# The taps of two channel tiles as four token phases on TensorE, and the second modulation columns on VectorE

## The chip, the cores and the metric

The kernel runs on one core of a Trainium2 chip. A core has TensorE (PE, the matrix multiplies), VectorE (DVE), ScalarE (ACT), GpSimd (POOL) and SyncE (SP), which mostly issues DMAs; POOL issues DMAs too. The metric is the device time of one execution in microseconds (us).

## The reference

Two residual layers on 1024 tokens of 1024 channels, then one RMSNorm. Layer 0 mixes tokens with a convolution module, layer 1 with sliding means; each is followed by a SwiGLU feed-forward part. The change lies in layer 0:

```python
def modulate(h, shift, scale):
    return h * (1.0 + scale[:, None, :]) + shift[:, None, :]

def conformer_conv(h, w1, b1, w_dw, b_dw, ln_g, ln_b, w2, b2):
    u = h @ w1 + b1
    a, g = jnp.split(u, 2, axis=-1)
    u = a * jax.nn.sigmoid(g)
    u = lax.conv_general_dilated(u, w_dw[:, None, :], window_strides=(1,),
        padding=[(CONV_WIDTH - 1, 0)], feature_group_count=D_MODEL) + b_dw
    u = jax.nn.silu(layer_norm(u, ln_g, ln_b))
    return u @ w2 + b2

    mod = c_act @ ada_w[i] + ada_b[i]          # c_act = silu(c), 6 x 1024 values
    sh_m, sc_m, g_m, sh_f, sc_f, g_f = jnp.split(mod, N_ADA, axis=-1)
    h = modulate(rms_norm(x, norm_mix_g[i]), sh_m, sc_m)
    ...
    x = x + (1.0 + g_m)[:, None, :] * y
    h = modulate(rms_norm(x, norm_ffn_g[i]), sh_f, sc_f)
    y = swiglu_ffn(h, ffn_w_gate[i], ffn_w_up[i], ffn_w_down[i])
    x = x + (1.0 + g_f)[:, None, :] * y
```

So each channel of the gated values `u` is convolved along the tokens with its own 31 taps (CONV_WIDTH). The layer norm over channels needs the taps of all channels of a token, and the feed-forward part's input `h` needs the scale `sc_f`.

## The kernel before

Channels lie on the 128 partitions, tokens along the free axis. There are two token chunks of 512, A and B, and eight channel tiles of 128, 0 to 7. A float32 product is made of three matmuls: each operand is split into a high and a low part, and `products` multiplies high by high, high by low and low by high. A weight is loaded by SP into a `raw` tile (3 buffers) and split into a `w` tile (5 buffers). ACT makes the high part (CAST w<-raw). For the low part a "summed" weight lets ACT write the negative copy (ACTIVATE w<-raw), to which a DMA of POOL's queue adds the weight again (w<-in_...); a "direct" one lets DVE subtract (TENSOR_TENSOR w<-raw,w).

Layer 0 in the order of PE's matmuls, by the names of their outputs: `a` and `g` are the two halves of `h @ w1` of one tile and chunk; first all of chunk A, and tiles 6 and 7 of B with those of A; then B's tiles 0 and 1; then `tap`, the taps that PE does; then B's tiles 2 to 5 with chunk A's layer norm between them (`mean`, `var`, `rstd`, one matmul or eight small ones each); `y`, the product with w2 for chunk A; B's last tile, and in it the norm of the feed-forward part for A (`var`, `rstd` again); then `p`, the first products of the feed-forward part, which read that norm's `h`.

The taps of a tile and chunk are 31 multiply-adds of shifted copies. VectorE does them into an accumulator `ca`; ACT and POOL share them (`pr` is a product by ACT, POOL sums into `pa`); a class `Taps` hands them out. Of chunk A PE does all 31 taps of tile 7 and 15 of tile 6: a tap there is a diagonal 128 x 128 weight (six weights `wdg` of up to eight diagonals), three matmuls of 482 to 512 columns, 138 in all. ACT reads tile 7's result from PSUM and adds the bias (u<-tap,vecs); tile 6's is added to VectorE's part. Chunk B's taps of both tiles are done by VectorE, ACT and POOL.

The modulation of layer 0 comes in columns, j = 0 to 5. For j = 2, 3 and for the second set, j = 4, 5 (the feed-forward scale and gate), PE multiplies `c` by the loaded columns (`ada`, `ada_columns`): of a column's eight row blocks, four matmuls each; two blocks are 16 records in the trace (each matmul counts twice), called a pair below; and at a column's end two transposing matmuls (`adac`). Other columns are done by VectorE in "dots" (`ada_task`): the loaded 128 x 1024 block times `cact`, summed along the free axis into one column of `mod`, eight dots a column. `adaw` tiles have 2 buffers (ADA_BUFS), so a load waits for the use of the one two before it. Behind column 4, POOL adds the bias and makes the scale (`mod`, `gains`); the first operation of the norm, t<-x,gains,rstd, reads it.

PE runs in the order in which the program is written; on the other engines a scheduler sets the order from the program, its priorities and manual dependencies. A planner keeps a clock for each engine; `pace` gives out steps of the waiting tasks to VectorE and POOL up to where PE's clock stands. `finish` and units such as `scale_done` force a task to its end. `mean_rsqrt` makes a norm's root (about eight small VectorE operations on `col` and `var`); operations in the list `recent`, the last 6 dots among them (RECENT), get a manual dependency that puts them behind the root.

Of the kernel before, what the change touches and what calls it, by code (L numbers as in the profile page):

```python
# [52 lines left out]
PE_TAPS = {6: 15, 7: CW}  # L53
# [46 lines left out]


def tap_groups(p):

    n = PE_TAPS[p]

    todo = list(range(CW - 1, -1, -1) if n == CW else range(CW - 3, CW - 3 - 2 * n, -2))
    return [todo[i : i + DIAGS] for i in range(0, len(todo), DIAGS)]
# [26 lines left out]
def trunk(ctx, tc, xT, c, vec, ada, adan, w1f, w1, wdg, w2, wgu, wdn, wds, wpl, out):  # L134
# [210 lines left out]
    kinds_d = [{q: [dram.tile([P, 2, 2, 512], F32, name=f"kinds_{l}_{q}_{b}") for b in range(3)] for q in BY_SEVEN[l]} for l in range(DEPTH)]  # L345
    KINDS = {"t1": (0, 0), "b22": (0, 1), "t3": (1, 0), "t2": (1, 1), "b11": (2, 0), "t4": (2, 1)}
# [55 lines left out]
    def ada_task(l, js, pause=None, first=None):  # L402

        def gen():
            todo = [(j, k) for j in js for k in range(KT)]
            ws = [ada_load(ada[(l * 6 + j) * KT + k], soft) for j, k in todo[:ADA_BUFS]]
            for i, (j, k) in enumerate(todo):
                yield first if first and i == 0 else pause or ("next" if "pooled" in st else "slow")
                ada_dot(ws.pop(0), l, j, k)
                if i + ADA_BUFS < len(todo):  # L410
                    j2, k2 = todo[i + ADA_BUFS]
                    ws.append(ada_load(ada[(l * 6 + j2) * KT + k2], soft))
                if k == KT - 1:
                    ada_post(l, j, 0, KT, G_)
                    ada_done.add((l, j))
# [324 lines left out]
    def conv_glu(ch, p, ba, bg, own=False):  # L740
        u = st["u", ch.i, p]
# [21 lines left out]
    def conv_in(*todo, fine=4):  # L763

        def emit(take):
            got = {}
            for each in todo:
# [4 lines left out]
                conv_u(ch, p)  # L772
# [10 lines left out]
                if ch.i == 0 and PE_TAPS.get(p, 0) < CW:  # L783
                    T["taps", 0, p] = Taps(A, p)
                if ch.i == 0 and p == KT - 1:
                    for q in PE_TAPS:
                        if PE_TAPS[q] < CW:
                            split_u(q)
# [3 lines left out]
    def split_u(p):  # L792

        u = st["u", 0, p][:, HALO - 2 : HALO - 2 + A.n]
        hi, lo = st["us", p] = pair("h0", "us")
        S_.copy(hi, u)
        either(A.n).tensor_tensor(lo, u, hi.bitcast(F32), op=SUB)

    def pe_taps(p):


        groups = tap_groups(p)
        us = []
        for i, js in enumerate(groups):
            def emit(take, i=i, js=js):
                if i == 0:
                    st["tap", p] = bank("tap")
                b, wt = st["tap", p], take()
                for q, j in enumerate(js):
                    full = PE_TAPS[p] == CW  # L810
                    o = (CW - 1 - j) // 2 * 2 if full else CW - 3 - j
                    c = j + o if full else 0
                    products(b[:, o:], wt, q, [v[:, c : c + A.n - o] for v in st["us", p]], j == groups[0][0], j == groups[-1][-1])
                    if q % 4 == 3:
                        pace()
                if i == len(groups) - 1:
                    if full:
                        S_.activation(st["u", 0, p][:, HALO:], b, AF.Identity, bias=V("conv_bdw", p))
                        st["taps", 0][p] = True
                    else:  # L820
                        T["taps", 0, p].other = b
            us.append((emit, wdg[sum(len(tap_groups(q)) for q in PE_TAPS if q < p) + i]))
        return us

    class Taps:
# [5 lines left out]
        def __init__(self, ch, p):  # L831
            self.ch, self.p, self.done, self.urgent = ch, p, False, False
            self.acc, self.part, self.other = None, None, None

            others = tap_groups(p) if ch.i == 0 and p in PE_TAPS else []
            self.todo, self.awaits = [j for j in range(CW - 1) if not any(j in js for js in others)], bool(others)
            tasks.append(self)

        def step(self, e):
# [43 lines left out]
            if e != "V" or self.awaits and self.other is None:  # L883
# [5 lines left out]
            if self.awaits:  # L889
                V_.tensor_tensor(d, d, self.other, op=ADD)  # L890
# [1136 lines left out]
    unit(lambda take: finish(*(T["taps", 0, p] for p in range(KT) if PE_TAPS.get(p, 0) < CW)))  # L2027
# [229 lines left out]
```

## Time and profile before

| | |
|---|---|
| time, median of 3 runs | 1676.87 us (1676.09 to 1678.81) |
| profiled execution, its own time | 1675.66 us |
| its span | 1673.9 us |
| PE busy | 1651.8 us (99%), 7550 matmul records |
| DVE, ACT, POOL busy | 1310.0 (78%), 804.1 (48%), 487.4 us (29%) |
| DMA | 378.60 MB, mean 226 GB/s |

A row of a timeline reads: start, duration, engine, line, operation, output<-inputs, the shape, the count, and in brackets the idle time ahead of it with what ended it. Rows of a kind that overlap or follow at once are joined into one with a count; its duration reaches from the first start to the last end, and a matmul's end is modelled, so the start of the next row says more than the sum of durations. L151 and L128 are helpers that record every operation, so groups are told apart by the names of tiles. The table by stages gives for each engine the busy time and the count. A row on a DMA issue gives the size and the median time from issue to landing.

### The profile page before, as it was taken

How to read it: one execution, taken by the hardware profiler on the slowest of the kernel's cores; microseconds unless marked ns; L12 is line 12 of the kernel's file. 1: busy time of each engine (PE TensorE's matmuls, PEld its weight loads, DVE VectorE, ACT ScalarE, POOL GpSimd, SP SyncE). 2: the span in 40 equal slices, each digit the busy share in tenths (PEclk: the TensorE clock that was granted, in tenths of full speed). 3: DMA queues.
4: the chain of work that ended last, by engine and by line, in shares of the span. 5: the costliest groups of instructions: out<-in, count | busy, mean ns of one | idle time of the engine just before them, and what ended most of it. 6: DMA issues, size and time to landing. Idle time of an engine off the chain costs nothing.

```text
span 1673.9 us, 21194 instructions
## 1 busy us (share of the span) xinstructions
PE 1651.8 (99%) x7550; PEld 1351.2 (81%) x7550; DVE 1310.0 (78%) x1867; ACT 804.1 (48%) x1090; POOL 487.4 (29%) x567
## 2 busy tenths in 40 slices
PE   7999999999999999999999999999999999999997
PEld 5777878787888888888888888888888888888887
DVE  8889899799759888888678957848777766658657
ACT  3669696867546332332234436637322222244354
POOL 3587777796002111221100502101111111000013
PEclk9999999999999999999999999999999999999999
DMA  8958997828776888886965959866777776686664
GB/s 301 295 176 228 225 236 205 226 78 241 229 234 168 278 264 287 282 272 206 400 231 164 285 155 283 247 211 199 189 225 222 220 227 183 207 273 207 192 170 126
DMA packets 117180, 378.60 MB, mean 226 GB/s; under 512 B 12369, under 2 KB 14545, under 8 KB 117074
## 3 DMA queue, kind: packets, MB, share of 16 engines
q1 hardware_dynamic: 79664, 245.63, 41.6%
q0 software_dynamic: 36832, 131.09, 32.5%
q8 instruction: 59, 0.97, 0.2%
q10 hardware_dynamic: 578, 0.53, 0.1%
q14 instruction: 47, 0.39, 0.1%
HBM read 310.61 MB, written 62.39 MB: 223 GB/s over the span
## 4 chain that ended last, share of the span: by engine, by line
PE 88%; POOL 3%; DVE 2%; DMA 2%; issue 2%; ACT 2%; DVEq 0%; SPq 0%; POOLq 0%; ACTq 0%
PE a L151 24%; PE dn L151 23%; PE e L151 14%; PE p L151 10%; PE y L151 6%; POOL pa L128 3%; PE first L151 3%; PE g L151 2%; PE tap L151 2%; DMA adaw<-in_adan_dram 1%; DMA s<-in_wds_dram 1%; PE ada L151 1%; ACT w L128 1%; DMA w<-in_wgu_dram 1%; PE var L151 1%
## 5 line engine op out<-in xcount | busy, mean ns | idle before, releaser
L128 ACT CAST w<-raw 128x1024 fp32r<-128x1024 f32 (+1 forms) x247 | 254.6, 1033 | 305.5 <-PE dn L151 56.9
L128 DVE TENSOR_TENSOR w<-raw,w 128x1024 fp32r<-128x1024 f32 (+1 forms) x173 | 209.3, 1214 | 62.2 <-ACT w L128 61.9
L151 PE MATMUL a<-n,w 128*128 128x512 f32 x1056 | 246.8, 389 | 0.2
L151 PE MATMUL p<-h,w 128*128 128x512 f32 x1056 | 243.7, 390 | 1.2 <-DMA w<-in_wgu_dram 1.0
L128 POOL TENSOR_TENSOR pa<-pa,pr 128x512 f32<-128x512 f32 x159 | 225.3, 1500 | 29.0 <-ACT pr L128 23.7
L151 PEld LDWEIGHTS p<-h,w 128*128 128x128 f32 x1056 | 197.3, 188 | 43.7 <-DMA w<-in_wgu_dram 1.4
L151 PEld LDWEIGHTS a<-n,w 128*128 128x128 f32 x1056 | 198.0, 188 | 42.2 <-DVE r L128 1.1
L151 PE MATMUL dn<-hi,w 128*128 128x512 f32 (+1 forms) x768 | 226.2, 377 | 0.4 <-DVE w L128 0.4
L151 PE MATMUL dn<-g,w 128*128 128x512 f32 x864 | 199.1, 390 | 0.2 <-DVE x L128 0.2
L151 PEld LDWEIGHTS dn<-g,w 128*128 128x128 f32 x864 | 161.7, 188 | 34.7 <-DVE x L128 0.6
L128 DVE SCALAR_TENSOR_TENSOR ca<-u,vecs,ca 128x512 f32<-128x512 f32 x246 | 170.6, 747 | 0.5
L151 PEld LDWEIGHTS dn<-hi,w 128*128 128x128 f32 x768 | 141.2, 188 | 27.0 <-DVE w L128 0.9
L151 PE MATMUL dn<-lo,w 128*128 128x512 f32 (+1 forms) x384 | 144.3, 376 | 0.0
L151 PE MATMUL a<-t,w 128*128 128x512 f32 x528 | 123.3, 389 | 0.0
L151 PE MATMUL e<-t,w 128*128 128x512 f32 x528 | 123.3, 389 | 0.0
L151 PE MATMUL e<-b,w 128*128 128x512 f32 x528 | 123.3, 389 | 0.0
L128 ACT ACTIVATE pr<-u,vecs 128x512 f32<-128x512 f32 x159 | 108.4, 717 | 25.0 <-POOL pa L128 19.7
L151 PEld LDWEIGHTS a<-t,w 128*128 128x128 f32 x528 | 99.1, 188 | 20.7
L151 PEld LDWEIGHTS e<-t,w 128*128 128x128 f32 x528 | 99.1, 188 | 20.6
L151 PEld LDWEIGHTS e<-b,w 128*128 128x128 f32 x528 | 99.1, 188 | 20.6
L1191 POOL DMA_DIRECT2D raw<-in_wgu_dram x41 | 36.5, 889 | 271.5 <-DVE r L128 104.2
L128 ACT CAST hi<-op 128x1024 fp32r<-128x1024 f32 (+1 forms) x52 | 48.5, 935 | 87.1 <-PE dn L151 77.2
(191 smaller groups left out, 2449.4 us busy)
## 6 DMA issues: line engine op xcount, KB each, us to landing
raw<-in_wgu_dram SPq DMA_DIRECT2D x132, 512.0 KB, 4.7
raw<-in_wds_dram SPq DMA_DIRECT2D x48, 512.0 KB, 6.0
adaw<-in_ada_dram POOLq DMA_DIRECT2D x48, 512.0 KB, 6.8
kinds<-k POOLq DMA_DIRECT2D x42, 512.0 KB, 7.7
raw<-in_wgu_dram POOLq DMA_DIRECT2D x41, 512.0 KB, 7.3
raw<-in_w_dram SPq DMA_DIRECT2D x36, 512.0 KB, 6.6
op<-kinds SPq DMA_DIRECT2D x36, 512.0 KB, 4.8
adaw<-in_adan_dram SPq DMA_DIRECT2D x32, 512.0 KB, 5.5
```

The lines of the kernel that those rows point to most:

```text
L128: self.last = self.order(getattr(self.eng, name)(out, *args, **kw))
L151: last_mm[0] = nc.tensor.matmul(out, lhsT, rhs, start=start, stop=stop, skip_group_check=more).ins.name
L1191: d = order(nc.gpsimd.dma_start(w[i], wgu[l, fp, src], accum_op=ADD))
```

## The change

**Taps.** PE now does all 31 taps of tiles 6 and 7, for both chunks. The tokens of a tile are dealt out in four phases (token modulo 4), and a matmul's 128 rows are 4 phases of 32 channels; so a tile gives four groups of 32 channels with 256 columns (1024 tokens / 4) each. A weight holds for each channel a 4 x 4 table of taps, from phase to phase, and nine shifts by a column (NM) cover the 31 taps: 2 tiles x 4 groups x 9 = 72 weight blocks, 9 `wdg` weights of eight, three matmuls of 256 columns for each block, 216 in all. Of the 9 weights those with even numbers are direct, the others summed.

The data changes its place through DRAM: the gated values go into a tile `ny` ordered by phase, by one DMA to `phased_d`; four or eight DMAs bring them into `us` with the phases on partitions; ACT makes the high part and DVE the low one. Results are copied by ACT into `acc`, stored to `tapped_d`, loaded by four DMAs for each tile and chunk into `ny`, and ACT's activation puts them back in order with the bias. All these DMAs are SP's. B's tile 0 now stands ahead of the taps on PE, tile 1 behind them; the return of B's tiles 6 and 7 is a unit behind tile 1. `Taps` no longer handles tiles 6 and 7.

**Modulation.** The second set, j = 4 and 5, is no longer PE's: `ada_task` makes 16 dots on VectorE of it, with loads on SP's queue.

```diff
-PE_TAPS = {6: 15, 7: CW}
+ON_PE = (6, 7)
+PHASES = 4
+GC = P // PHASES
+NM = (CW - 1 + 2 * (PHASES - 1)) // PHASES
+LEAD = NM - 1
+SEG = 2 * WSLOT // PHASES
 DIAGS = 8
...
-    def ada_task(l, js, pause=None, first=None):
+    def ada_task(l, js, pause=None, first=None, queue=soft):
...
-            ws = [ada_load(ada[(l * 6 + j) * KT + k], soft) for j, k in todo[:ADA_BUFS]]
+            ws = [ada_load(ada[(l * 6 + j) * KT + k], queue) for j, k in todo[:ADA_BUFS]]
...
     def conv_glu(ch, p, ba, bg, own=False):
-        u = st["u", ch.i, p]
+        u = st.get(("u", ch.i, p))
...
+        if p in ON_PE:
+            phased(ch, p, ba, sg)
             return
...
+    def phased(ch, p, ba, sg):
+
+        n = ch.n // PHASES
+        t = temp(ch.n, "ny", 2)
+        V_.scalar_tensor_tensor(t.rearrange("p (f n) -> p f n", f=PHASES), ba.rearrange("p (n f) -> p f n", f=PHASES), V("conv_b1", p),
+                                sg.rearrange("p (n f) -> p f n", f=PHASES), op0=ADD, op1=MUL)
+        d = phased_d[p][ch.i]
+        sync.dma_start(d.rearrange("p f n -> p (f n)"), t)
+        if ch.i == 0:
+            st["us", p] = phase_parts(p)
+        o = LEAD + ch.i * n
+        view = d.rearrange("(g c) f n -> f c g n", c=GC)
+        for gs, hi, lo in st["us", p]:
+            for f in range(PHASES):
+                sync.dma_start(lo[GC * f : GC * f + GC, : len(gs), o : o + n].bitcast(F32), view[f][:, gs[0] : gs[-1] + 1])
+            at = (slice(None), slice(0, len(gs)), slice(o, o + n))
+            S_.copy(hi[at], lo[at].bitcast(F32))
+            V_.tensor_tensor(lo[at], lo[at].bitcast(F32), hi[at].bitcast(F32), op=SUB)
+
+    def pe_taps():
+
+        blocks = [(p, g, m) for p in ON_PE for g in range(PHASES) for m in range(NM)]
...
+                for q, (p, g, m) in enumerate(these):
+                    if m == 0 and g % 2 == 0:
+                        st["tap"] = bank("tap")
...
+                    products(b[:, g % 2 * n : g % 2 * n + n], wt, q, (hi, lo), m == 0, m == NM - 1, more=True)
                     if q % 4 == 3:
                         pace()
...
+                    if m == NM - 1 and g % 2:
+                        out_ = temp(2 * n, "acc", 2)
+                        S_.copy(out_, b)
+                        sync.dma_start(tapped_d[p][:, g - 1 : g + 1], out_.rearrange("p (g n) -> p g n", g=2))
+                        if g == PHASES - 1:
+                            tapped(A, p)
...
+            units_.append((emit_of(blocks[i : i + DIAGS]), wdg[i // DIAGS] if i // DIAGS % 2 else direct(wdg[i // DIAGS])))
...
+    def tapped(ch, p):
...
+        t = temp(ch.n, "ny", 2).rearrange("p (f n) -> p f n", f=PHASES)
+        view = tapped_d[p].rearrange("(f c) g n -> g c f n", f=PHASES)
+        for g in range(PHASES):
+            sync.dma_start(t[GC * g : GC * g + GC], view[g][:, :, ch.i * n : ch.i * n + n])
+        S_.activation(u[:, HALO:].rearrange("p (n f) -> p n f", f=PHASES), t.rearrange("p f n -> p n f"), AF.Identity, bias=V("conv_bdw", p))
+        st["taps", ch.i][p] = True
...
-    for p in rest[: len(rest) - HOLD - HOLD_LN]:
+    first, *others = rest[: len(rest) - HOLD - HOLD_LN]
+    conv_in((B, first))
+    for u in pe_taps():
+        unit(*u)
+    for p in others:
         conv_in((B, p))
-    for p in PE_TAPS:
-        for u in pe_taps(p):
-            unit(*u)
+    unit(lambda take: [tapped(B, p) for p in ON_PE])
...
     def ada_second(take):
-        T["ada_f"] = Task(ada_columns((4, 5)), False, 0)
-        T["ada_f"].free = True
+        T["ada_f"] = ada_task(0, (4, 5), queue=sync)
     unit(ada_second)
-    taps(B, *some, *rest[: len(rest) - HOLD - HOLD_LN])
+    taps(B, *rest[: len(rest) - HOLD - HOLD_LN])
```

How the change stands in the engines' orders, at the two places where PE waits for them (a row: line of the helper, operation, output<-inputs with buffer numbers, and the engines or DMA queues that it waits for).

ACT ahead of the copy of chunk A's mean, before; u_988 is tile 7 of A, w_1954 and w_2100 are weights of the coming `a` and `g`:

```order
L128 ACTIVATE u_988<-tap_1779,vecs 128x512 [waits PE_49]
L128 CAST w_1954<-raw_1952 128x1024 [waits DMAHW0_49,DMASW7_49]
L128 ACTIVATE w_1954<-raw_1952 128x1024
L128 CAST w_2100<-raw_2098 128x1024 [waits DMAHW1_49,DMASW0_49,PE_49]
L128 ACTIVATE w_2100<-raw_2098 128x1024
L128 COPY ny_2012<-mean_2010 128x512 [waits PE_49]
L128 ACTIVATE acc_2022<-u_672 128x512 [waits DVE_49]
```

The same place of the change; u_994 is tile 7 of A and u_2097 tile 7 of B, w_2228 a weight that takes the buffer of the `a` matmuls ahead of `mean`:

```order
L125 CAST w_2228<-raw_2226 128x1024 [waits DMAHW6_49,DMASW6_49,PE_49]
L125 ACTIVATE w_2228<-raw_2226 128x1024
L125 ACTIVATE u_994<-ny_1994,vecs 128x512 [waits DMAHW7_49,DMAHW1_49,DMAHW0_49]
L125 ACTIVATE u_2097<-ny_2104,vecs 128x512 [waits DMAHW4_49,DMAHW5_49,DMAHW3_49,DMAHW2_49]
L125 COPY ny_2157<-mean_2155 128x512 [waits PE_49,Activation_49]
L125 ACTIVATE acc_2167<-u_678 128x512 [waits DVE_49]
```

The activation of A's tile 7 has moved behind the weight whose cast waits for PE, and B's tile 7 has come in ahead of the copy of the mean. The loads of ny_2104 wait for ACT (the activation of u_994, whose tile was in that buffer), and on PE mean_2155 waits for the sum of u_994 on VectorE.

VectorE from the root of the feed-forward part's norm on, before:

```order
L128 SCALAR_TENSOR_TENSOR col_2845<-var_2840,col_2845 128x4 [waits DVE_49]
L128 TENSOR_TENSOR var_2840<-var_2840,col_2845 128x4 [waits DVE_49]
L128 SCALAR_TENSOR_TENSOR var_2840<-var_2840,col_2845 128x4 [waits DVE_49]
L128 SCALAR_TENSOR_TENSOR col_2845<-var_2840,col_2845 128x4 [waits DVE_49]
L128 SCALAR_TENSOR_TENSOR t_2894<-x_79,gains,rstd_2889 128x512 [waits PE_49,Pool_49]
L128 SCALAR_TENSOR_TENSOR t_2898<-x_79,gains,rstd_2889 128x512 [waits Pool_49]
L128 SCALAR_TENSOR_TENSOR h_2801<-t_2894,mod,h_2801 128x512 [waits Activation_49]
```

The same place of the change:

```order
L125 TENSOR_TENSOR var_2920<-var_2920,col_2925 128x4 [waits DVE_49]
L125 SCALAR_TENSOR_TENSOR var_2920<-var_2920,col_2925 128x4 [waits DVE_49]
L125 SCALAR_TENSOR_TENSOR col_2925<-var_2920,col_2925 128x4 [waits DVE_49]
L125 SCALAR_TENSOR_TENSOR adaw_2441,mod<-adaw_2441,cact 128x1024 [waits DMAHW6_49]
L125 SCALAR_TENSOR_TENSOR adaw_2529,mod<-adaw_2529,cact 128x1024 [waits DMAHW0_49]
L125 SCALAR_TENSOR_TENSOR adaw_2623,mod<-adaw_2623,cact 128x1024 [waits DMAHW1_49,DVE_49]
L125 SCALAR_TENSOR_TENSOR adaw_2719,mod<-adaw_2719,cact 128x1024 [waits DMAHW3_49,DVE_49]
L125 SCALAR_TENSOR_TENSOR adaw_2815,mod<-adaw_2815,cact 128x1024 [waits DMAHW4_49,DVE_49]
L125 SCALAR_TENSOR_TENSOR adaw_2877,mod<-adaw_2877,cact 128x1024 [waits DMAHW5_49,DVE_49]
L125 SCALAR_TENSOR_TENSOR t_2972<-x_79,gains,rstd_2967 128x512 [waits PE_49,Activation_49,Pool_49]
L125 SCALAR_TENSOR_TENSOR t_2976<-x_79,gains,rstd_2967 128x512
```

Six dots, the third to the eighth of column 4, have come in between the end of the root (col_2925) and the first operation of the norm; one and two stand earlier, within `y`. Their loads, on SP, with the weight loads around them:

```order
L495 DMA raw_3076<-in_wgu_dram 128x1024 [waits DMAHW5_49,DMAHW0_49,DVE_49]
L166 DMA adaw_2623<-in_ada_dram 128x1024 [waits DVE_49]
L495 DMA raw_3128<-in_wgu_dram 128x1024 [waits DMAHW6_49,Activation_49]
L166 DMA adaw_2719<-in_ada_dram 128x1024 [waits DVE_49]
L166 DMA adaw_2815<-in_ada_dram 128x1024 [waits DVE_49]
L166 DMA adaw_2877<-in_ada_dram 128x1024 [waits DVE_49]
L166 DMA adaw_2880<-in_ada_dram 128x1024 [waits DVE_49]
L166 DMA adaw_2883<-in_ada_dram 128x1024 [waits DMAHW7_49,DVE_49]
L166 DMA adaw_2956<-in_ada_dram 128x1024 [waits DMAHW0_49,DVE_49]
```

Here adaw_2623 is the load of the fifth dot; each load waits for VectorE, the dot two before it.

More of the change, by code (lines that the diff above doesn't have):

```diff
@@ L411, in gen @@
                     j2, k2 = todo[i + ADA_BUFS]
-                    ws.append(ada_load(ada[(l * 6 + j2) * KT + k2], soft))
+                    ws.append(ada_load(ada[(l * 6 + j2) * KT + k2], queue))
                 if k == KT - 1:
@@ L782, in emit @@
                 conv_glu(ch, p, *b, fine < 4)
-                if ch.i == 0 and PE_TAPS.get(p, 0) < CW:
+                if ch.i == 0 and p not in ON_PE:
                     T["taps", 0, p] = Taps(A, p)
[L785 to L788, printed above, removed]
         tiles = list(dict.fromkeys(e[1] for e in todo if e))
         unit(emit, *[w1[p, i] for p in tiles for i in range(2)])
[L792 to L813, printed above, removed]
+    def phase_parts(p):
+        if p == ON_PE[0]:
+            hi, lo = (wpair(B, "us", F32R).rearrange("p a (b w) -> p (a b) w", w=SEG) for _ in range(2))
+            parts = [(range(PHASES), hi, lo)]
+        else:
+            parts = [(range(o, o + 2), block("h0", "us"), block("h0", "us")) for o in range(0, PHASES, 2)]
+        for _, hi, lo in parts:
+            for part in (hi, lo):
+                G_.memset(part[:, :, :LEAD].bitcast(F32), 0.0)
+        return parts
@@ L832, in __init__ @@
             self.ch, self.p, self.done, self.urgent = ch, p, False, False
-            self.acc, self.part, self.other = None, None, None
-            others = tap_groups(p) if ch.i == 0 and p in PE_TAPS else []
-            self.todo, self.awaits = [j for j in range(CW - 1) if not any(j in js for js in others)], bool(others)
+            self.acc, self.part = None, None
+            self.todo = list(range(CW - 1))
             tasks.append(self)
@@ L882, in step @@
                 return True
[L883 removed]
+            if e != "V":
                 return False
@@ L2019, in trunk @@
     rest = list(range(KT - 1 - SHARE))
[L2020 removed]
+    first, *others = rest[: len(rest) - HOLD - HOLD_LN]
[3 more added lines that the diff above has]
+    for p in others:
         conv_in((B, p))
[L2022 to L2024 removed]
+    unit(lambda take: [tapped(B, p) for p in ON_PE])
     unit(lambda take: held.__setitem__(0, True))
     unit(lambda take: finish(T["ada", 0]))
[L2027 removed]
+    unit(lambda take: finish(*(T["taps", 0, p] for p in range(KT) if p not in ON_PE)))
     def ada_second(take):
[L2030 to L2031 removed]
+        T["ada_f"] = ada_task(0, (4, 5), queue=sync)
     unit(ada_second)
[L2033 removed]
+    taps(B, *rest[: len(rest) - HOLD - HOLD_LN])
     for p in rest[len(rest) - HOLD - HOLD_LN : len(rest) - HOLD]:
```

62 lines of the change are left out of this document (31 added, 31 removed).

## The prediction

> **What bounds the kernel now.** I read the busy shares of the page first, then PE's waits by releaser, then the busy time by stage, then PE's timeline of the stages touched.
>
> ```profile
> span 1673.9 us, 21194 instructions
> PE 1651.8 (99%) x7550; PEld 1351.2 (81%) x7550; DVE 1310.0 (78%) x1867; ACT 804.1 (48%) x1090; POOL 487.4 (29%) x567
> ...
> PE var L151 <- DVE acc L128: 4.9, 1, 4.9
> ```
>
> PE is the bound and its longest wait is 4.9 us, at the start. By stage (columns: us, then busy time of PE, PEld, DVE, ACT, POOL; PEclk, DMA share, GB/s):
>
> ```profile
> 65.00:345.00 280.00, 279.66 (x1419) 217.13 (x1418) 250.96 (x389) 221.84 (x312) 215.61 (x192) 1.00 0.80 218
> 345.00:1600.00 1255.00, 1253.28 (x5556) 1035.74 (x5555) 955.75 (x1305) 520.69 (x686) 228.06 (x312) 1.00 0.74 229
> ```
>
> From 65 to 345 us, the stages of the change, PE has 0.3 us idle. So PE work taken out there is gained in full unless a new wait appears, work taken from VectorE gains nothing by itself, and a wait put in is lost in full: behind 345 us only 1.7 us of 1255 are idle, so nothing later makes it up.
>
> **PE work removed.** PE's timeline of chunk A's taps now, and of matmuls with 256 columns in the last stage:
>
> ```profile
> 167.31 5.76 PE L151 MATMUL tap<-us,w 128*128 128x512 f32 x24
> 173.00 0.64 PE L151 MATMUL ada<-adaw,ccols 128*32 128x256 f32 x8
> ...
> 181.16 0.51 PE L151 MATMUL adac<-quarters,t 128*128 128x4 f32 x4
> 181.52 18.61 PE L151 MATMUL tap<-us,w 128*128 128x508 f32 x81
> 199.97 5.62 PE L151 MATMUL a<-h,w 128*128 128x512 f32 x24
> ```
>
> ```profile
> 1647.24 0.28 PE L151 MATMUL dn<-lo,w 128*128 128x256 f32 x1
> ...
> 1649.40 0.28 PE L151 MATMUL dn<-lo,w 128*128 128x256 f32 x1
> ```
>
> From 167.31 to 199.97 are 32.66 us; less some 0.9 for the ada and adac records among them (181.16 to 181.52 is 0.36) the 138 tap matmuls took 31.7. In the second fence 18 matmuls of 256 columns lie between the two rows, 2.16 us, so 0.12 each although each has its own weight load. 216 x 0.12 = 25.9; if this stage runs 4% slower than the last one, 27.0. I take **-5.3** (-5.8 to -4.7).
>
> The second set's 16 columns were 8 pairs on PE; a pair costs 1.00 (292.38 to 293.38 below) and each of the two adac 0.36: **-8.7**. By place: 3 pairs before y starts (-3.0), 2 pairs and an adac within y (-2.4), 1 pair in the norm (-1.0), 2 pairs and an adac behind it (-2.4). All in all -14.0.
>
> What VectorE, ScalarE and POOL lose (the taps of both chunks' two tiles that were theirs) and get (the phases' casts, 16 dots of 1.2 us) lies beside PE and is counted only where PE waits for it; without that cover it would be VectorE's 251 of 280 us in the stages above that sets the time, with 29 to spare.
>
> **Weights of the taps.** Four of the nine units have their low part added by POOL's queue; its DMA issues (KB each, us to landing):
>
> ```profile
> raw<-in_wdg_dram SPq DMA_DIRECT2D x6, 512.0 KB, 6.9
> w<-in_wdg_dram POOLq DMA_DIRECT2D x6, 512.0 KB, 9.3
> ```
>
> Load, cast (1 us) and addition take 6.9 + 1 + 9.3 = 17 us from the first issue; a unit now takes PE only 24 x 0.12 = 2.9 us, so the five weight buffers reach 14.4 us ahead. A wait of 0 to 3 us in all; I take **+1.3**, about half. The data's own way (store, 8 loads, two casts) has B(0)'s 11 us of matmuls and, for tile 7, another 13 of tile 6 over it; I cost it at nothing. Without that cover it is a store and a load of 3.8 us each (row below) in front of the taps.
>
> **The layer norm of chunk A.** PE, ACT and DVE now, and two kinds of DMA issues (KB each, us to landing):
>
> ```profile
> 205.43 1.02 PE L151 MATMUL mean<-acc,ones 128*128 128x512 f32 x2
> 218.45 0.95 PE L151 MATMUL var<-ones,acc 128*128 128x1 f32 x8
> 225.88 1.16 PE L151 MATMUL rstd<-ident,col 128*128 128x128 f32 x8
> 238.91 11.58 PE L151 MATMUL y<-v,w 128*128 128x512 f32 x48
> ```
>
> ```profile
> 200.17 0.69 ACT L128 ACTIVATE u<-tap,vecs 128x512 f32<-128x512 f32 x1 [1.42 <-PE tap L151]
> 205.63 1.05 ACT L128 CAST w<-raw 128x1024 fp32r<-128x1024 f32 x1 [2.87 <-PE a L151]
> 207.54 0.57 ACT L128 COPY ny<-mean 128x512 f32<-128x512 f32 x1
> ```
>
> ```profile
> 208.14 3.08 DVE L128 TENSOR_TENSOR u<-u,mean 128x512 f32<-128x512 f32 x5 [3.29 <-ACT ny L128]
> 216.76 0.69 DVE L128 SCALAR_TENSOR_TENSOR acc<-t,acc 128x512 f32<-128x512 f32 x1
> k<-kept SPq DMA_DIRECT2D x14, 256.0 KB, 3.8
> out_dram<-x SPq DMA_DIRECT2D x4, 128.0 KB, 2.2
> ```
>
> Call E the end of a just ahead of mean (205.43 now). The rows of ACT shown with the change say that tile 7's activation of A now stands on ACT behind a weight cast that waits for that same a, and mean waits for it. From E: 0.2 until the cast starts, 1.9 for its two instructions (205.63 to 207.54), 0.7 for the activation, 0.7 for the addition on DVE: mean **waits 3.5 to 3.7**. Now mean follows a at once. Behind that activation four loads for B's tile 7 are issued (0.3 us each; landing in 2.2 to 3.8, the last two rows), and the copy of the mean stands on ACT behind the activation that waits for them: E + 2.8 + 1.3 + 2.2 to 3.8 + 0.7 + 0.6 = 7.6 to 9.2. DVE starts its subtractions there (2.7 behind E now) and ends the sum of squares 9.3 later (208.14 to 217.45), at E + 16.9 to 18.5. PE reaches var at E + 3.6 + 0.5 + two groups of 5.65 = 15.4, so it **waits another 1.5 to 3.1**; the 1.0 us between 217.45 and 218.45 was all the slack there was. Together **+5.9** (5.0 to 6.8; below it 0, if the loads and the cast come early; above it 9 with landings of 6 us). From var to rstd PE has 7.4 us of work, the root below takes 2.6: rstd and y follow unhindered.
>
> So y starts 5.3 + 3.0 - 1.3 - 5.9 = 1.1 us earlier than now: what the taps gain, the layer norm takes back but for that.
>
> The strided accesses I cost at nothing. By the Trainium skill (SBUF — State Buffer, "Door 1: The DMA port swizzle") accesses that leave a 16-byte line of SBUF, or an 8-byte one of PSUM, each time pay a penalty; the GLU now reads PSUM at every fourth float and the activation its tile in steps of 512 bytes. No run here shows such an operation; if each took twice its time, the two activations would add some 1.4 us to the chain above, and the time would be 1684.7.
>
> **The norm behind y.** PE and DVE now:
>
> ```profile
> 290.03 0.95 PE L151 MATMUL var<-ones,acc 128*128 128x1 f32 x8
> ...
> 292.38 1.07 PE L151 MATMUL ada<-adaw,ccols 128*32 128x256 f32 x16
> 293.38 1.67 PE L151 MATMUL g<-h,w 128*128 128x512 f32 x6
> ...
> 299.89 4.92 PE L151 MATMUL p<-h,w 128*128 128x512 f32 x21
> ```
>
> ```profile
> 291.09 1.41 DVE L128 SCALAR_TENSOR_TENSOR ca<-u,vecs,ca 128x512 f32<-128x512 f32 x2
> ...
> 293.81 0.16 DVE L128 SCALAR_TENSOR_TENSOR col<-var,col 128x4 f32<-128x4 f32 x1
> 296.06 1.41 DVE L128 SCALAR_TENSOR_TENSOR t<-x,gains,rstd 128x512 f32<-128x512 f32 x2 [2.09 <-PE rstd L151]
> ```
>
> Groups (busy, mean ns) of the dots and of what follows them on POOL, then landings, of the window 280 to 330 and of the tile adaw:
>
> ```profile
> L128 DVE SCALAR_TENSOR_TENSOR adaw<-adaw,cact 128x1024 f32<-128x1024 f32 x64 | 77.5, 1215 | 0.7 <-DMA adaw<-in_ada_dram 0.7
> L128 POOL TENSOR_SCALAR gains<-mod 128x8 f32<-128x8 f32 x7 | 2.8, 397 | 3.3 <-DVE mod L128 3.0
> ```
>
> ```profile
> adaw<-in_adan_dram SPq DMA_DIRECT2D x6, 512.0 KB, 3.9
> DMA to landing us min/median/max: 3.4/6.2/13.6
> ```
>
> The rows of DVE and SP shown with the change put dots 3 to 8 behind the root (the col row at 293.81) and ahead of the first t, and each load from the fifth on waits for the dot two before it. Count from the root's end T0. Dots 3 and 4 have their data: 1.2, 2.4. Load 5 goes at 1.3 and lands, with the 3.9 of the window 280 to 330, at 5.3; dot 5 ends 6.5, dot 6 7.8. Load 7 goes at 6.7, lands 10.6; dot 7 11.8, dot 8 13.1. Three small POOL instructions of 0.4 make scale of it: 14.6 with the handing over. Then two t (16.0), dot 9, whose load lands at 16.0 (17.2), and the first low part of h (0.7, as one t): 18.0. PE has 299.89 - 290.03 = 9.9 us of work from var to p, 8.9 without the ada pair. The root now ends 3.9 behind the start of var with two taps of 0.66 in it, which the order no longer has there: 2.6. So from T0 PE has 6.2 us of work. p's second matmul reads that low part, so PE **waits 11.6**. With every landing at the 3.4 of the last row 10.2; at the median 6.2, 18.2; if no load were waited for at all, six dots, POOL, two t, dot 9 and h end at T0 + 12.1, a wait of 5.7. I take the 3.9 since it is of this very stage and the queues are emptier while PE stands. Behind the loads on SP waits one weight load, due 28 us into p: free.
>
> PE also restarts slowly. At the start, after its waits, the windows (us, PE busy and matmuls, PEclk, DMA) show
>
> ```profile
> 18.95:22.40 3.45, 3.45 (x7) 1.00 0.26 103
> 22.40:26.00 3.60, 3.60 (x15) 1.00 0.73 245
> ```
>
> 0.49 us each and then 0.24, so 1.7 us lost: **+1.7** behind the wait of 11.6. The column of the clock does not show it.
>
> By the Trainium skill (TensorE: Matmul & The Clock Gate, "Part 1: The HAM clock gate (the "warmup" mystery)") an idle window of some 3.4 us halves PE's clock for about as long; the 3.45 us above agree. By that rule the 3.6 us wait of mean may cost 1.7 once more, and the time would be 1685.0.
>
> **Sum:** -5.3 + 1.3 - 3.0 + 5.9 - 2.4 - 1.0 - 2.4 + 11.6 + 1.7 = **+6.4**. The profiled execution took 1675.66 (span 1673.9 and 1.76 around it), 1.2 under the median of 1676.87; on it 1682.1, on the median **1683.3**.
>
> **Rivals.**
> Layer norm without waits (not slower): the way through DRAM is back early and ACT is ahead of my count, so 5.9 + 1.3 fall away: -0.8, 1676.1. It decides if the activation is done before E. Against it: the weight cast ahead of it is bound to E by its buffer. Chance 0.15.
> Dots without waits for loads: the wait is 5.7 and its slow restart perhaps 1.0: -0.2, 1676.7. Against it: two buffers, and no load has landed under 3.4. Chance 0.10.
> Nothing waits: -14.0, 1662.9. For it only that PE is the bound now; the rows of ACT and of DVE speak against it. Chance 0.05.
> Slow landings: 6.2 in place of 3.9 in the norm (+6.6) and 3 us in the taps (+1.7): +14.7, 1691.6. For it the median of all adaw loads; POOL's sums in front of the scale would act alike. Chance 0.17.
> That the change doesn't do what it says is excluded by the order.
>
> **Chances.** The forecast has 0.50, with its own range 1679 to 1688; 0.03 is for what I don't see. A measurement here can't tell less than 0.2% (3.4 us) from no change: slower, above 1680.2, are the forecast but for 0.05 and the slow landings, 0.62; same are that 0.05, most of the two middle rivals and a part unseen, 0.25; faster 0.13. The range 1671 to 1692 leaves out the last rival's upper half and the case without waits.
>
> **What would show it.** In the profile after: tap in 26 to 28 us; PE waits at mean of 3.6 and at var of 2 to 3; one PE wait of 10 to 14 ahead of the first p, released by DVE or ACT, with dots 3 to 8 between root and t and DVE idle on adaw's DMA; the first 3.4 us behind it hold 7 matmuls, not 15. No wait above 5 us at p would make the forecast wrong, and so would y starting before 234.

## The result, and the profile after

| | before | the change |
|---|---|---|
| time, median | 1677.62 us (4 runs, 1676.09 to 1678.81) | 1722.3 us (4 runs, 1719.58 to 1723.32) |
| ratio | | 1.0264, 95% interval 1.0247 to 1.0282 |
| span of the profiled execution | 1673.9 us | 1717.8 us |

The change makes the kernel 44.7 us slower. The direction was forecast, the size was not: 6.4 us were forecast, and the range ended at 1692. The head of the page of the change:

```profile
span 1717.8 us, 21128 instructions
...
PE 1647.7 (96%) x7492; PEld 1353.5 (79%) x7492; DVE 1311.4 (76%) x1838; ACT 805.4 (47%) x1088; POOL 479.5 (28%) x552
```

PE is busy for 4.1 us less and idle for 48 us more. The forecast took 14.0 us of work from it; so, as an estimate from these two, some 10 us of its busy time are matmuls that ran slower (the mean granted clock is 0.985, before 0.998). What it waits for, from the view of PE's waits (us in total, times, longest):

```profile
PE mean L148 <- DVE acc L125: 22.1, 2, 12.7
PE p L148 <- ACT h L125: 14.7, 1, 14.7
PE var L148 <- DVE acc L125: 5.2, 1, 5.2
PE tap L148 <- DVE us L125: 3.5, 1, 3.5
...
PE dn L148 <- DVE g L125: 2.5, 3, 1.6
```

(The var of 5.2 is the one at the start, 4.9 before.) The same waits in PE's timeline:

```profile
200.70 5.60 PE L148 MATMUL a<-h,w 128*128 128x512 f32 x24
219.03 2.05 PE L148 MATMUL mean<-acc,ones 128*128 128x512 f32 x2 [12.73 <-DVE acc L125]
...
250.61 6.00 PE L148 MATMUL y<-v,w 128*128 128x512 f32 x22
...
323.92 0.79 PE L148 MATMUL p<-h,w 128*128 128x512 f32 x1 [14.72 <-ACT h L125]
325.63 46.35 PE L148 MATMUL p<-h,w 128*128 128x512 f32 x191 [0.92 <-DVE h L125]
...
428.51 2.08 PE L148 MATMUL mean<-acc,ones 128*128 128x512 f32 x2 [9.42 <-DVE acc L125]
```

Starts of the same work in both traces give the account:

| work on PE | before | after | later by | forecast |
|---|---|---|---|---|
| `a` ahead of chunk A's mean | 199.97 | 200.70 | 0.7 | -4.0 |
| first `y` of A | 238.91 | 250.61 | 11.7 | -1.1 |
| first `p` | 299.89 | 323.92 | 24.0 | 7.1 |
| first `y` of chunk B | 449.92 | 491.63 | 41.7 | 6.4 |
| end of the span | 1673.9 | 1717.8 | 43.9 | 6.4 |

From the first p to chunk B's y are another 17.7 us, where nothing was forecast but a slow restart and the 2.4 of ada and adac removed. They are 0.9 of a second wait at p, 2.9 of a slow clock behind it, 4.2 in the first `dn` group, 9.4 at chunk B's mean and 2.7 in the products around that, less the 2.4. Behind chunk B's y only 2 us follow. So the loss lies in three places: chunk A's mean, the first p, and chunk B's mean with the products around it.

### The profile page after: what moved, and what is told of

Its sections match the earlier page's. It is cut to its first block, busy times and chain, and to the rows that moved or that the text cites. A ratio compares the mean times of both kernels' runs of the same rounds, so it can differ in the third digit from the quotient of the medians.

```text
span 1717.8 us, 21128 instructions
## 1 busy us (share of the span) xinstructions
PE 1647.7 (96%) x7492; PEld 1353.5 (79%) x7492; DVE 1311.4 (76%) x1838; ACT 805.4 (47%) x1088; POOL 479.5 (28%) x552
## 3 DMA queue, kind: packets, MB, share of 16 engines
q0 software_dynamic: 36544, 130.04, 31.2%
## 4 chain that ended last, share of the span: by engine, by line
PE 81%; DMA 6%; DVE 5%; ACT 3%; issue 2%; POOL 2%; SPq 0%; DVEq 0%; POOLq 0%; ACTq 0%
PE a L148 23%; PE dn L148 22%; PE e L148 14%; PE p L148 10%; PE y L148 6%; PE first L148 3%; PE g L148 2%; POOL pa L125 2%; ACT w L125 1%; DVE ca L125 1%; DMA raw<-in_w_dram 1%; DMA adaw<-in_adan_dram 1%; DVE w L125 1%; DMA raw<-in_wdn_dram 1%; DVE adaw L125 1%
## 5 line engine op out<-in xcount | busy, mean ns | idle before, releaser
L125 DVE TENSOR_TENSOR w<-raw,w 128x1024 fp32r<-128x1024 f32 (+1 forms) x178 | 222.3, 1253 | 65.4 <-ACT w L125 64.9
L148 PE MATMUL p<-h,w 128*128 128x512 f32 x1056 | 249.1, 396 | 16.8 <-ACT h L125 14.7
L148 PEld LDWEIGHTS p<-h,w 128*128 128x128 f32 x1056 | 200.9, 191 | 61.0 <-ACT h L125 15.1
L125 POOL TENSOR_TENSOR pa<-pa,pr 128x512 f32<-128x512 f32 x148 | 218.8, 1524 | 42.3 <-ACT pr L125 39.0
L125 DVE SCALAR_TENSOR_TENSOR ca<-u,vecs,ca 128x512 f32<-128x512 f32 x188 | 130.2, 745 | 0.2
L125 DVE SCALAR_TENSOR_TENSOR adaw<-adaw,cact 128x1024 f32<-128x1024 f32 x80 | 104.5, 1311 | 11.0 <-DMA adaw<-in_ada_dram 11.0
L125 ACT ACTIVATE pr<-u,vecs 128x512 f32<-128x512 f32 x148 | 100.9, 716 | 22.9 <-POOL pa L125 16.2
```

The source lines that it names most:

```text
L125: self.last = self.order(getattr(self.eng, name)(out, *args, **kw))
L148: last_mm[0] = nc.tensor.matmul(out, lhsT, rhs, start=start, stop=stop, skip_group_check=more).ins.name
```

## The experiments

Times are medians; "+" is against the runs of the kernel before on the same chip (medians 1676.6 to 1677.8).

### The two halves apart

`dots_only` is the kernel before with only the second modulation set moved, `taps_only` the change without it:

```diff
 # dots_only, on the kernel before (with ada_task's queue as in the change)
-        T["ada_f"] = Task(ada_columns((4, 5)), False, 0)
-        T["ada_f"].free = True
+        T["ada_f"] = ada_task(0, (4, 5), queue=sync)
 # taps_only, on the change
-        T["ada_f"] = ada_task(0, (4, 5), queue=sync)
+        T["ada_f"] = Task(ada_columns((4, 5)), False, 0)
+        T["ada_f"].free = True
```

> The kernel before with only the second modulation set moved to VectorE; taps as before. Theory Q (the time went into waits that the order of single queues makes, each priced where it stands): -8.7 of PE work, one wait of 12 to 15 us at the first p with a slow restart of 1.7, chunk B's mean waits little: 1680 to 1686. Theory L (VectorE is overloaded in this part of the program: what it is given, or loses while it waits, comes out again as a wait of chunk B's mean): the same wait at p and 8 to 10 us at chunk B's mean: 1690 to 1697.

> The change with only its taps; the second modulation set stays on PE as before. Theory Q: -5.3 of tap work, a wait of 3.5 at the first tap and of 12.7 at chunk A's mean with a slow restart, no wait at the first p, and at chunk B's mean none, since VectorE has 58 taps less: about 1689. Theory L: the time that VectorE loses behind chunk A's mean comes back at chunk B's mean too: 1695 to 1700.

`dots_only`: 1713.37, ratio 1.0216 (1.0201 to 1.0231), +35.8. `taps_only`: 1694.45, ratio 1.0103 (1.0088 to 1.0118), +16.9. Both lose, the dots twice as much as the taps. The dots alone are far over both expectations: the wait at p is as expected, 12.5, but chunk B's mean comes 38 us later than before (some 12 of it, since 54 more products stand ahead of it) and its first y 32. PE's timeline, before and in `dots_only`:

```profile
416.66 1.10 PE L151 MATMUL mean<-acc,ones 128*128 128x512 f32 x2
```

```profile
454.58 1.13 PE L151 MATMUL mean<-acc,ones 128*128 128x512 f32 x2 [0.97 <-DVE acc L128]
...
482.20 0.80 PE L151 MATMUL y<-v,w 128*128 128x512 f32 x1 [4.05 <-ACT v L128]
```

Theory L had VectorE's lateness, but not its place and too small a size: at the mean itself PE waits 1.0, and the rest is in the products on both sides of it. In `taps_only` chunk B's mean waits for nothing, as theory Q said, though the time lies between the two theories; the waits there are at the first tap and at chunk A's mean:

```profile
PE mean L148 <- DVE acc L125: 12.3, 1, 12.3
...
PE tap L148 <- DMA raw<-in_wdg_dram: 4.0, 1, 4.0
```

Alone the halves add up to 52.7, together they cost 44.7. The likely reason, not tested by itself: the taps take work from VectorE (busy 1291.4 us in `taps_only`, 1310.0 before), and the dots fill that room (1311.4 in the change).

### Mending the two orders that the prediction blamed

`dots_free` takes the dots out of the list that is put behind the root; `tapB_late` brings chunk B's way back behind B's tile 3; `late_free` does both:

```diff
 # dots_free, late_free
         T["ada_f"] = ada_task(0, (4, 5), queue=sync)
+        T["ada_f"].dots = False
 # tapB_late, late_free
-    unit(lambda take: [tapped(B, p) for p in ON_PE])
...
         conv_in((B, p))
+        if i == 1:
+            unit(lambda take: [tapped(B, q) for q in ON_PE])
         taps(B, p)
```

> The change, but the dots of the second set are not put behind the norm's root; they then stand one by one within y and ahead of the root. Theory Q: the wait at the first p (14.7 and 0.9 with a slow restart of 1.7) is gone, the others stay: about 1704, and 1695 if chunk B's mean then waits no more. Theory L: the dots push chunk B's taps back, its mean waits as long or longer: 1704 to 1712.

> The change, but the way back of chunk B's tiles 6 and 7 (loads and activations) stands behind B's tile 3 instead of tile 1, so that on ScalarE no activation of B stands ahead of chunk A's mean. Theory Q: the wait at chunk A's mean falls from 12.7 to 0 to 4, and its slow restart with it: 1709 to 1713. Theory L: VectorE's taps of chunk B gain nothing by it and the time is given back behind: 1717 to 1722.

> Both mends of order on the change together: chunk B's way back behind B's tile 3, and the dots not behind the root. Theory Q: their waits go (14.7 at p, some of 12.7 at the mean): 1693 to 1700. Theory L: as the dots alone not behind the root, since VectorE's time decides behind them: 1707 to 1713.

`dots_free`: 1710.86, ratio 1.02 (1.0183 to 1.0217), 11.4 less than the change. The wait of 14.7 at p is gone (what stays there is 1.5 in two), but chunk B's mean waits 11.8 and not 9.4. `tapB_late`: 1722.06, ratio 1.026 (1.0244 to 1.0276): nothing gained. Chunk A's mean waits 9.1 and not 12.7, but the kernel reaches the tap stage 2 us later, and 2.4 at var and 1.6 at y come instead. `late_free`: 1713.04, ratio 1.0206 (1.0187 to 1.0225); its two means wait 9.9 and 10.1. Theory L comes nearest in all three (two lie less than 0.1 above its range): the wait at p is real, and two thirds of what it cost stay away when it is mended; the rest is given back where VectorE is late.

The same mend in the kernel that has the dots alone:

```diff
 # dots_only_free, on dots_only
+        T["ada_f"].dots = False
```

> The kernel before with only the second set on VectorE, its dots not behind the root of the norm. Theory L: the wait of 12.5 at the first p is gone with its slow restart, but the waits around chunk B's mean (some 20 us) stay: 1693 to 1700. Theory Q: they were the echo of the wait at p and go with it: 1670 to 1680.

1708.78, ratio 1.0183 (1.0168 to 1.0198), +31.0. The waits around chunk B's mean stay and are larger than theory L had them; they are no echo of the wait at p.

### VectorE's time by itself

`ballast` leaves the kernel before as it is and adds 48 small VectorE operations that nobody waits for; `ballast_half` adds 24 of them:

```diff
...
+    def ballast():
+        G_.memset(extra, 0.0)
+        for i in range(16):
+            yield "slow"
+            for _ in range(3):                 # ballast_half: only where i is odd
+                V_.scalar_tensor_tensor(extra, extra, 1.0, cact[:, :232], op0=MUL, op1=MUL, accum_out=unused[:, i : i + 1])
...
         T["ada_f"].free = True
+        T["extra"] = Task(ballast(), False, 0)
```

> The kernel before with the second set on PE as it was, and 16 times three small VectorE operations (some 19 us in all) given to the same planner at the place of the dots: nobody waits for them, they load nothing. Theory L (VectorE's time is what the dots cost, beside the wait at the norm): chunk B's mean and the products around it wait, 1690 to 1700. Theory Q (only waits for loads and results cost): 1677 to 1681.

> As the ballast of 16 times three small VectorE operations in the kernel before (+38.6 us), but with 8 times three, half of it (some 16 us of VectorE's time). If VectorE has no room in these stages, half the load costs half: 1693 to 1699. If there is room first (it was idle for 29 of 280 us) and a point from which it decides, much less than half: 1678 to 1686.

`ballast`: 1716.34, ratio 1.0226 (1.0209 to 1.0243), +38.6. `ballast_half`: 1710.73, ratio 1.0194 (1.0176 to 1.0212), +33.5. No DMA, no wait at the first p, and yet as much lost as with the dots, and more than the 1690 to 1700 of theory L. Half the count costs more than half, which neither reading expected. Groups of DVE from 200 to 470 us (busy, mean ns of one) say why a count is the wrong measure. The weights' subtraction before, for comparison:

```profile
L128 DVE TENSOR_TENSOR w<-raw,w 128x1024 fp32r<-128x1024 f32 x21 | 29.4, 1404 | 5.9 <-ACT w L128 5.8
```

The change:

```profile
L125 DVE SCALAR_TENSOR_TENSOR ca<-u,vecs,ca 128x512 f32<-128x512 f32 x83 | 58.3, 745 | 0.2
L125 DVE SCALAR_TENSOR_TENSOR adaw<-adaw,cact 128x1024 f32<-128x1024 f32 x16 | 27.0, 1692 | 9.0 <-DMA adaw<-in_ada_dram 9.0
```

`dots_only`:

```profile
L128 DVE SCALAR_TENSOR_TENSOR adaw<-adaw,cact 128x1024 f32<-128x1024 f32 x16 | 31.2, 1963 | 6.2 <-DMA adaw<-in_ada_dram 6.1
```

`ballast`, then `ballast_half`:

```profile
L128 DVE SCALAR_TENSOR_TENSOR extra<-extra,cact 128x232 f32<-128x232 f32 x48 | 37.3, 777 | 0.2
```

```profile
L128 DVE TENSOR_TENSOR w<-raw,w 128x1024 fp32r<-128x1024 f32 x18 | 32.3, 1792 | 0.0
...
L128 DVE SCALAR_TENSOR_TENSOR extra<-extra,cact 128x232 f32<-128x232 f32 x24 | 24.3, 1013 | 0.1
```

The 64 dots of the kernel before took 1.20 to 1.23 us each, the 16 here 1.69 to 1.96 in the mean; an operation of the ballast takes 0.38 at the least and 1.01 in the mean of `ballast_half`; w<-raw,w takes 1.79 there and 1.40 before. The taps `ca`, whose accumulator lies in PSUM, take 745 ns everywhere. The groups that get much longer read two operands from SBUF, and they do so beside POOL, whose sums `pa` take some 1.5 us each: in `ballast` the 15 operations that started while no operation of POOL was under way took 0.38 to 0.40 us, the other 33 0.90 in the median. How much time a run adds to VectorE is therefore read from its busy time over the whole profile, which also has the operations that got longer and the 7 to 15 sums that the planner gave to POOL in place of VectorE's taps. Against the kernel before (1310.0 busy in a span of 1673.9), in the profiled executions:

| run | VectorE busy | span |
|---|---|---|
| `ballast` | +43.3 | +43.1 |
| `ballast_half` | +28.8 | +29.8 |
| `dots_only` | +31.9 | +37.1 |
| `dots_only_free` | +28.1 | +33.1 |

(The profiled execution of `ballast_half` was its fastest, 5 us under the median.) In `dots_only` VectorE also stands idle 6.2 us for the dots' loads. Not all of the price is waiting: in `ballast` PE is idle 29.0 us more, and 14.1 us more busy with the same 7550 matmuls, at a mean granted clock of 0.989 and not 0.998.

The last run keeps the ballast's place in every engine's order and changes only the operation:

```diff
-                V_.scalar_tensor_tensor(extra, extra, 1.0, cact[:, :232], op0=MUL, op1=MUL, accum_out=unused[:, i : i + 1])
+                V_.tensor_scalar(extra, extra, 1.0, 0.0, op0=MUL, op1=ADD, accum_out=unused[:, i : i + 1])
```

> The ballast of 16 times three VectorE operations again (+38.6 us), in the same place of every engine's order, but with one operand from SBUF instead of two. In the ballast an operation took 0.78 us in the mean and 0.38 at the least, as the dots of the change took 1.69 and not 1.22. Theory P (an operation with two operands in SBUF waits for POOL's; one with a single operand does not; and the price follows VectorE's real time): 0.4 us each, some 18 us of VectorE's time less, 1690 to 1702. Theory O (the price comes from the order, the planner having moved taps and products): 1711 to 1718, whatever the operations take. By the Trainium skill (SBUF — State Buffer, "Who interferes with whom") a VectorE instruction with two SBUF inputs contends with a GpSimd one that reads SBUF, and one with at most one input outside the faster modes doesn't.

1702.06, ratio 1.016 (1.0142 to 1.0179), +25.5:

```profile
L128 DVE TENSOR_SCALAR_CACHE_REDUCE extra<-extra 128x232 f32<-128x232 f32 x48 | 18.4, 384 | 0.2
```

With one operand from SBUF each takes its 0.38 us. VectorE has 18.9 us less to do than in `ballast` (18.4 for 37.3), and 13.1 of the loss go. That is theory P, at the upper edge of what it gave, and it excludes theory O: in the two traces the operations of every engine come in the same order. What stays, 25.5, is near the 22.2 us that the 48 operations and the reads of their accumulators (3.8) still take, and nearer to what VectorE's busy time gained over the kernel before, 26.2 with a span of +26.8. So VectorE's time in these stages costs about its own length, with no room first. How much of the +25.5 is the planner's, which gave POOL 13 more sums than before, wasn't separated.

### The way through DRAM

`taps_actq` issues the results' stores and loads on ScalarE's queue, `no_return` leaves that way out (tokens are then out of order in chunk A, and chunk B's two tiles have other data), `taps_less_dma` leaves the weight additions of POOL's queue out from the first tap to chunk A's residual (the low parts are then wrong); all three on `taps_only`:

```diff
 # taps_actq (and the store alike)
-            sync.dma_start(t[GC * g : GC * g + GC], view[g][:, :, ch.i * n : ch.i * n + n])
+            act.dma_start(t[GC * g : GC * g + GC], view[g][:, :, ch.i * n : ch.i * n + n])
 # no_return, in tapped
-        t = temp(ch.n, "ny", 2).rearrange("p (f n) -> p f n", f=PHASES)
...
+        t = (x[1][p] if ch.i else b).rearrange("p (f n) -> p f n", f=PHASES)
 # taps_less_dma, in load_weight; "light" from the first tap to chunk A's residual
-            order(nc.gpsimd.dma_start(low ..., src, accum_op=ADD))
+            if not st.get("light"):
+              order(nc.gpsimd.dma_start(low ..., src, accum_op=ADD))
```

> The change with only its taps (the second modulation set on PE), and the results' stores and loads through DRAM on ScalarE's queue instead of SP's. In the run with the taps alone a load of 64 KB landed 8 us after its issue. Theory R (they stand behind 512 KB weights in SP's queue): on a queue of their own they land in 2 to 4 us, the wait at chunk A's mean falls from 12.3 to 3 to 6: 1683 to 1688. Theory D (the DMA engines are full, whatever the queue): landings of 7 us and more, wait at the mean 10 or longer: 1691 to 1698.

> The change with only its taps, and the results' way back through DRAM left out: chunk A's two tiles take their bias from PSUM as before (tokens then out of order), chunk B's two take other data in the place of their result. If the way back is what chunk A's mean waits for: no wait there, 12.3 and a slow restart of 1.7 less, 1679 to 1682, that is still over the kernel before by the wait of 4 at the first tap. If the mean waits for VectorE's own taps anyway: a wait of over 5 stays, 1686 or more.

> The change with only its taps, and for the 15 weights loaded between the first tap and chunk A's return to its residual the low part's DMA left out (the low part then holds the negative weight), so that POOL's queue moves half a megabyte less for each. Theory D (the small loads land late because the DMA engines are full): loads of the results land in 5 us or less in the median instead of 8, the wait at chunk A's mean falls from 12.3 to 7 or less, 1689 or less. Rival (the way back is long by its own steps: the store, its landing, the issue behind others on SP, the load): landings and wait stay, 1692 to 1697.

`taps_actq`: 1697.91, ratio 1.012 (1.0105 to 1.0135). `no_return`: 1686.79, ratio 1.0057 (1.0042 to 1.0072). `taps_less_dma`: 1687.15, ratio 1.006 (1.0042 to 1.0078). The wait at the mean and the landings of the results, 176 to 222 us, of `taps_actq` and then of `taps_less_dma`:

```profile
PE mean L148 <- DVE acc L125: 17.4, 1, 17.4
...
ny<-tapped ACTq DMA_DIRECT2D x12, 64.0 KB, 8.1
```

```profile
PE mean L148 <- DVE acc L125: 5.0, 1, 5.0
...
ny<-tapped SPq DMA_DIRECT2D x16, 64.0 KB, 3.4
```

A queue of its own brings no faster landing (8.1; 6.6 in `taps_only`, the 8 in the expectation was another run's), and ScalarE, which now issues them, stands idle 3.8 us around the issues at 202 us. With POOL's weight additions away, the same loads on SP's queue land in 3.4 (and the 512 KB weights there in 4.7 and not 7.7), and the mean waits 5.0. That is theory D: they are late because the DMA engines are full. In `no_return` the mean waits 1.0, so it was the way back that it waited for; the way in then waits longer instead, with nothing behind it to hide that:

```profile
PE tap L148 <- DVE us L125: 7.5, 1, 7.5
```

That is 3.5 more than at the first tap of `taps_only`, most of the 4.8 by which 1682 was missed; the rest wasn't traced. No run came under the kernel before.

## Why the prediction was wrong

**The step that failed first: "lies beside PE and is counted only where PE waits for it".** The bound of the stages was read from PE's busy time alone, and the 29 us that VectorE was idle in 280 were taken for room. They are not. VectorE must have done all taps of chunk B by its mean, and before the change it was busy 87 of the 95 us around there (DVE, the third of the engines' times in the row), while PE waited for almost nothing:

```profile
345.00:440.00 95.00, 93.69 (x416) 76.14 (x415) 86.85 (x126) 61.27 (x88) 59.61 (x47) 1.00 0.52 160
```

The ballast shows it: VectorE's time put in there comes out at the end at about its length. So the dots had to be priced as VectorE's time: in `dots_only` 31.2 for the 16, 6.2 idle for their loads and 1.3 for reading the accumulators make 38.7, and the run cost 35.8. In the change the taps take from VectorE about what the dots bring, and its busy time is the same (1311.4 and 1310.0); there it loses by standing idle: from 200 to 345 us it is busy 108.5 of 145 us, before 128.4. What lies behind p the prediction looked at only for room to make a wait up (1.7 idle of 1255). Nothing did make it up, but new waits came there, 9.4 at chunk B's mean above all.

**"1.2" for a dot.** The row that it was taken from is a mean over the 64 dots of the kernel before, none of which took over 1.23. The 16 of the change took 1.69 in the mean. The Trainium skill (SBUF — State Buffer, "Who interferes with whom") says that a VectorE instruction with two SBUF inputs contends with a GpSimd one that reads SBUF; the dots, the ballast and the run with one operand agree with it, 777 ns against 384. It is a rule that spoke against this change, and the prediction hadn't weighed it.

**"The layer norm of chunk A": +5.9 forecast, 12.7 and a slow restart measured.** In the prediction mean waits 3.6, for the cast of a weight that stands on ScalarE ahead of the activation of A's tile 7, and var another 1.5 to 3.1, for the way back of B's tile 7 behind that activation. In the trace the whole wait is at mean, and var has none. Two steps failed. First, tile 7's own result was taken to be there by then: its way back through DRAM was put at nothing. Its store, issued at 195.80, landed after 9.8 us, and the last of its loads, issued at 206.08, at 213.6, that is 7.3 us behind the end of `a` at 206.3. Second, the loads of B's tile 7 don't wait for that activation (at 216.99), as read from the order, but for the one of B's tile 6: they were issued from 210.92 on, so they had landed in time. Where no activation of B stands ahead, in `tapB_late`, ScalarE waits for the loads of A's tile 7 alone, and the mean still 9.1:

```profile
216.59 1.17 ACT L125 ACTIVATE u<-ny,vecs 128x512 f32<-128x512 f32 x1 [7.54 <-DMA ny<-tapped]
```

The landing of such loads was sized from rows of quieter stages, 2.2 to 3.8. ScalarE, VectorE and the DMAs of the change there:

```profile
199.36 1.05 ACT L125 ACTIVATE w<-raw 128x1024 fp32r<-128x1024 f32 x1
209.72 1.17 ACT L125 ACTIVATE u<-ny,vecs 128x512 f32<-128x512 f32 x1 [9.31 <-DMA ny<-tapped]
210.80 0.66 ACT L125 ACTIVATE t<-g,vecs 128x512 f32<-128x512 f32 x1
```

```profile
211.50 0.75 DVE L125 SCALAR_TENSOR_TENSOR u<-a,vecs,t 128x512 f32<-128x512 f32 x1 [10.76 <-ACT t L125]
```

```profile
ny<-tapped SPq DMA_DIRECT2D x14, 64.0 KB, 7.7
tapped<-acc SPq DMA_DIRECT2D x3, 256.0 KB, 7.5
```

The loads landed after 7.7 in the median; this stage had a DMA share of 0.92 before the change already (176 to 222 us). And of B's activations the one in the way was not the one counted, tile 7's ahead of the mean's copy, but that of B's tile 6, ten rows earlier in ScalarE's order. Behind it waited the sigmoid of a GLU, for that VectorE, and for VectorE's last taps the sum; it is what the change has over the 9.1 of `tapB_late`, some 3.6.

**"The norm behind y": 11.6 forecast, 14.7 and 0.9 measured.** The mechanism is the one described, dot by dot:

```profile
303.00 0.16 DVE L125 SCALAR_TENSOR_TENSOR col<-var,col 128x4 f32<-128x4 f32 x1
303.08 2.21 DVE L125 SCALAR_TENSOR_TENSOR adaw<-adaw,cact 128x1024 f32<-128x1024 f32 x1
...
310.41 1.22 DVE L125 SCALAR_TENSOR_TENSOR adaw<-adaw,cact 128x1024 f32<-128x1024 f32 x1 [2.89 <-DMA adaw<-in_ada_dram]
...
315.38 1.23 DVE L125 SCALAR_TENSOR_TENSOR adaw<-adaw,cact 128x1024 f32<-128x1024 f32 x1 [3.74 <-DMA adaw<-in_ada_dram]
...
320.19 1.23 DVE L125 SCALAR_TENSOR_TENSOR adaw<-adaw,cact 128x1024 f32<-128x1024 f32 x1 [2.35 <-DMA adaw<-in_ada_dram]
...
322.36 1.41 DVE L125 SCALAR_TENSOR_TENSOR t<-x,gains,rstd 128x512 f32<-128x512 f32 x2 [0.94 <-POOL gains L125]
```

The first t starts 19.2 us behind the root's end and not 14.6: dots 3 and 4 took 2.2 and 2.3 beside POOL, and the loads waited for landed in 4.5 in the median (300 to 325) and not 3.9. Undone, this wait gave back 11.4 of 44.7. (The prediction's own terms, 18.0 less 6.2, make 11.8 and not 11.6; with that its sum is 6.6, and nothing else changes.)

**"+1.3" for the taps' weights.** A wait of 3.5 came there, but for `us`, the data's way in, which was costed at nothing; in `taps_only` it was the first weight's load, 4.0. The taps themselves took what was forecast: 28.2 us without the wait and the ada records, of which 1.5 are a slow start behind that wait.

**The slow restart** was sized by one case of 1.7. After the wait at p it lasted twice as long. The windows show it, in the clock's column too (the last but two), which had stood at 1.00 in the prediction's case:

```profile
323.92:327.34 3.42, 2.50 (x5) 1.71 (x6) 3.42 (x6) 1.33 (x2) 0.00 (x0) 0.50 0.44 141
327.34:330.76 3.42, 3.42 (x9) 2.65 (x9) 3.42 (x6) 1.98 (x3) 0.00 (x0) 0.50 0.10 42
428.51:431.93 3.42, 3.42 (x6) 2.10 (x7) 1.30 (x3) 0.58 (x1) 0.00 (x0) 0.50 1.05 240
```

The third is behind chunk B's mean; behind chunk A's the column has 0.52. So each of the three waits of 9 us and more was followed by a stretch at half clock.

**Of the rivals**, slow landings came nearest, in its means and not in its size (1691.6). The case with the layer norm unhindered and the one without waits for loads are excluded by the trace.

## What to carry to other kernels

An engine that was 90% busy ahead of a deadline of the bounding engine was a bound here too, though the bounding engine showed no wait: before moving work onto such an engine, look at what has to be done by that deadline, and price the work at its length there. Ask also when a result that goes through DRAM is back; here it was taken to be there. Take an operation's duration, and a transfer's landing, from the stage in which it will run: the same dot took 1.2 and 1.7 us, the same 64 KB load 3.4 and 8, by what ran beside them. The way through DRAM, in a stage whose DMA share is 0.9, cost two landings of 7 us and more, on SP's queue and on ScalarE's.

## What the runs showed of the hardware that was not expected

VectorE operations with two operands in SBUF took up to 2.6 times as long beside POOL's sums (384 ns at the least against 1013 in the mean of `ballast_half`); the taps, with one operand in PSUM, took 745 ns throughout. Operations with strided accesses took half as long again and more: the activation that reads its tile in steps of 512 bytes, and the GLU that reads PSUM at every fourth float, against their plain forms (the first row is of the kernel before, the others of the change):

```profile
L128 ACT ACTIVATE u<-tap,vecs 128x512 f32<-128x512 f32 x1 | 0.7, 689 | 1.4 <-PE tap L151 1.4
```

```profile
L125 ACT ACTIVATE u<-ny,vecs 128x512 f32<-128x512 f32 x4 | 4.7, 1189 | 10.0 <-DMA ny<-tapped 9.3 <-issue 0.7
```

```profile
L125 DVE SCALAR_TENSOR_TENSOR ny<-a,vecs,t 128x512 f32<-128x512 f32 x4 | 4.6, 1141 | 0.0
...
L125 DVE SCALAR_TENSOR_TENSOR u<-a,vecs,t 128x512 f32<-128x512 f32 x7 | 5.2, 749 | 13.2 <-ACT t L125 13.2
```

The rule of the Trainium skill (SBUF — State Buffer, "Door 1: The DMA port swizzle") on 16- and 8-byte lines, cited in the prediction, had the sign of this; the factor is 1.7 for the activation and 1.5 for the GLU. The stride wasn't tested by itself: the plain activation reads PSUM and the strided one SBUF, and the GLU's second operand, in SBUF, is strided too. For loads on a queue of their own that still land late, the Trainium skill (DMA: Bandwidth & Descriptors, "Issuing engines are not separate DMA queues") says that DMAs of ScalarE, SyncE and GpSimd run on the same 16 DMA engines in the end, whichever engine started them; `taps_actq`, 8.1 us on ScalarE's queue, agrees.
